# All eight heads of a chunked RWKV-7 recurrence in one sequence of chunks per pass, on one Trainium2 core

## The chip, the core and the metric

The program runs on one core of a Trainium2 chip. The core's engines work side by side, each with its own in-order queue: TensorE (PE in the profile, its weight loads PEld) multiplies matrices into PSUM; VectorE (DVE), ScalarE (ACT) and GpSimd (POOL) do the element-wise work; SP issues the DMAs between HBM and the on-chip memory (SBUF). They wait for each other through semaphores. The metric is the device time of one execution in microseconds.

## What is computed

Two layers' worth of branches share one input: an RWKV-7 recurrence (eight heads of 64) and a sliding-window attention (eight query heads, two key heads, window 128). Both are gated, merged and added to the input. The prompt has 2048 tokens; eight single-token samples go through the same weights.

```python
mod = (jax.nn.silu(c) @ w_ada + b_ada)[:, None, :]
shift, scale, gate = jnp.split(mod, 3, axis=-1)
h = rms_norm(x, norm_g) * (1.0 + scale) + shift
u = h @ w_in
...
def step(S, inp):
    r_t, w_t, k_t, v_t, kk_t, a_t = inp
    sa = jnp.einsum('bhvk,bhk->bhv', S, -kk_t)
    S = (S * w_t[:, :, None, :] + sa[..., None] * (kk_t * a_t)[:, :, None, :]
         + v_t[..., None] * k_t[:, :, None, :])
    return S, jnp.einsum('bhvk,bhk->bhv', S, r_t)
S_fin, o = lax.scan(step, s0.astype(f32), (seq(r_h), seq(w_h), seq(k_h), seq(v_h), seq(kk), seq(a_h)))
...
y_a = o_a * jax.nn.silu(z_a)
y_b = o_b * jax.nn.silu(z_b)
merged = jax.nn.sigmoid(g_a) * (y_a @ w_o_a) + jax.nn.sigmoid(g_b) * (y_b @ w_o_b)
return x + gate * (merged @ w_out), wkv_new, shift_new, k_state, v_state
```

All of it is fp32. The recurrence is computed in chunks of 64 steps: inside a chunk the steps are solved at once by the inverse of a triangular 64x64 matrix for each head and chunk, and only the state goes from chunk to chunk.

## The kernel before

**Passes.** The tokens go in four passes of 512 columns, which are eight chunks of 64. One pass (pass 1) also carries the eight sample columns, in two pieces of 260.

**Dense tiles.** `dense` makes one tile of 128 rows of `u`. Each fp32 operand is split into a high and a low part, so a tile takes three matmuls for each of eight blocks, 24 matmuls of 128x512 in all (`mm3`, issued by `mm`, L579), into one PSUM bank of the kind d. Weight pages (`w`, 128x1024) come by DMA as high and low halves; in pass 0 the vector engines also split them. An epilogue on ScalarE or VectorE takes the tile out of the bank into a page of the kind p.

**The recurrence** runs for a group of four heads (two pairs of heads, `rwkv_group`), twice a pass:

- `prep_pair` makes the decays, the keys and the matrices of each chunk.
- `inverses` inverts the 32x32 diagonal blocks. The matrices go to HBM (`d1`) and come back as one page with a matrix a partition (`NL`, one place of the kind nl). An identity page `QL` is loaded from HBM (`in_idl`). Then 31 times a product and a sum (62 VectorE instructions) build the inverses, each step from the one before. The result goes to HBM (`d2`) in two stores and comes back in eight loads as `Q`. Four VectorE transposes make `T11` from it; then come two bursts of 64 32x32 matmul records each, with a copy (`YT`) between them, which fill the off-diagonal blocks.
- The chain goes over the eight chunks: matmuls with `W` (the state into the chunk, 128x64), a copy, matmuls with `Q` (64x64) and those inside the chunk (`within`), copies, matmuls with `BK` (the new state), and sums that make the state of the next chunk. The results gather in two PSUM banks `ops` of the kind g. After the eighth chunk they are split and normed.

**The order.** The code is run once to record all operations with what they read and write (`do` L538, `mm` L579, `mms` L597, `tr` L604, `dma` L613 are the lines that the profile names). `schedule` then lists them for the engines. A key orders them: the number of the dense tile at which an operation was recorded, times six, minus a lead from the table `LEADS`; the lowest key that is ready and has its places goes first. Places are counted by `CAPS`: 75 pages of SBUF (p), 11 s, 14 t, 8 weight pages (w), one nl, three dense PSUM banks (d) and five others (g). `places` gives an operation a place only if the operations recorded ahead of it can still get theirs:

```python
if b.first > front and int(live[b.kind][front:b.first].max()) + k >= caps[b.kind]:
    return None
```

So at a point where the recorded program itself fills all pages, nothing recorded later may take one. What comes out is one fixed list for each engine, and the engines follow it in order.

**What surrounds it.** In the main loop a pass records the first group's recurrence (`rwkv(0)`), then all of the attention (`attention()`, with its dense tiles kb, vb, q and zb), then the second group's (`rwkv(1)`), then the gates, the merge and the output tiles. Ahead of pass 0, `ada` makes the modulation: a group of columns either with split operands (matmuls of 18 columns) or whole in fp32 (9 columns, `whole`), by the table `ADA`.

Of the kernel before, what the change touches and what calls it, by code (L numbers as in the profile page):

```python
# [18 lines left out]
CH = 512  # L19
# [68 lines left out]
def _constants():  # L88
# [19 lines left out]
CAPS = {"p": 75, "s": 11, "t": 14, "w": 8, "nl": 1, "d": 3, "g": 5}  # L108
LEADS = {
    "prep": (2490.0, 3436.9, 460.9, 3438.6),  # L110
    "inv": (2996.1, 5954.0, 5871.1, 5871.1),
    "chain": (3475.6, 3475.6, 3475.6, 3475.6),
    "gn": (2855.6, 4741.8, 4539.0, 2629.7),
    "wd": (2207.5, 3240.1, 1705.2, 3248.2),
    "norm": (4852.3, 820.0, 820.0, 820.0),
    "att": (4680.1, 4726.2, 4352.4, 4642.8),
    "sample": (1285.3, 1285.3, 1562.2, 1562.2),
    "bias": (2948.2, 5008.5, 5008.5, 5008.5),
    "h": (3088.9, 3088.9, 3088.9, 3109.5),
    "x": (209.4, 253.7, 253.7, 253.7),  # L120
# [388 lines left out]
def hybrid_step_kernel(ctx: ExitStack, tc: tile.TileContext, A, O):  # L509
# [152 lines left out]
    xst = K([128, 8, NB], "xst")  # L662
# [3 lines left out]
    dma(xst, A["xsT"])  # L666
# [21 lines left out]
    sct = K([128, 8, 18], "sct", F32R)  # L688
    sc32 = K([128, 8, 9], "sc32")
# [129 lines left out]
    us = K([128, len(ORDER), NB], "us")  # L819
    kprev = [K([128, 128], f"kprev{i}", F32R) for i in range(4)]  # L820
# [86 lines left out]
    def dense(key, epi):  # L907

        wt = early.pop(key, None) or weights("w_in", INDEX[key])
        for c0, n in st["segs"]:  # L910
# [194 lines left out]
    def rwkv_group(q, g, rkv, lw, lx):  # L1105
# [616 lines left out]
```

## Time and profile before

| | us |
|---|---|
| median of 2 runs | 1904.93 |
| lowest, highest | 1904.24, 1905.62 |
| the profiled execution | 1904.95 |
| its span from first to last instruction | 1903.1 |

A row of the lines names the source line, the engine, the operation, the tile written and those read, the shape of the stationary operand (for matmuls), the output's shape, the count, then busy us and mean ns of one, and last the idle time of the engine in front of them with what ended it. A row of a timeline has the start, the time to the end of the last one, and how many; in brackets the engine's idle time ahead of it. Names have lost their numbers there: `p<-p,nl` is a page written from a page and from nl. fp32 matmuls with 32x32 and 64x64 operands leave two records each.

### The profile page before, as it was taken

The page shows a single profiled execution, that of the slowest core. Times are in us where ns is not written, and L with a number is a line of the kernel's source. Part 1 is how long each engine was busy: PE and PEld are TensorE (multiplying, and loading weights), DVE is VectorE, ACT ScalarE, POOL GpSimd, SP SyncE. Part 2 cuts the span into 40 slices and gives each one's busy share as a digit, 9 for nine tenths or more (in the row PEclk, how much of TensorE's full clock was granted, in tenths as well). Part 3 has the DMA queues.
Part 4 walks back from the last instruction along what each step waited for, and adds up shares of the span by engine and source line. Part 5 has one row for each costly group of instructions (what it writes and reads, how often), then busy time and mean ns, then how long its engine had stood idle before and what let it go on. Part 6 is the DMA issues. An engine that isn't in the chain of part 4 may idle for free.

```text
span 1903.1 us, 32620 instructions
## 1 busy us (share of the span) xinstructions
PE 1807.5 (95%) x12544; PEld 1444.5 (76%) x12544; DVE 1302.0 (68%) x3138; ACT 798.5 (42%) x1605; POOL 93.9 (5%) x170
## 2 busy tenths in 40 slices
PE   6899999999999799899999999999999999999999
PEld 2667666677799778798998786677788787677787
DVE  8889979459377869792835795964563885894351
ACT  6667545353157355323504544521422562651300
POOL 0000210000000001010000100100000000100000
PEclk9999999999999899999999999999999999999999
DMA  9475537667845413453676453145467454236355
GB/s 335 175 265 213 172 110 273 222 231 283 320 158 175 145 68 102 161 189 118 211 245 201 145 183 119 67 157 186 150 228 249 158 177 141 72 125 194 113 192 187
DMA packets 162456, 343.20 MB, mean 180 GB/s; under 512 B 65485, under 2 KB 69246, under 8 KB 162300
## 3 DMA queue, kind: packets, MB, share of 16 engines
q1 hardware_dynamic: 162300, 341.11, 52.6%
q8 instruction: 99, 1.62, 0.3%
q14 instruction: 57, 0.47, 0.1%
HBM read 263.09 MB, written 77.96 MB: 179 GB/s over the span
## 4 chain that ended last, share of the span: by engine, by line
PE 48%; DVE 18%; ACT 4%; DMA 2%; issue 1%; SPq 1%; DVEq 0%; ACTq 0%
PE d L579 39%; DVE p L538 17%; PE g L597 5%; ACT p L538 3%; PE g L579 2%; PE g L604 2%; ACT L538 1%; DMA p<-in_xT 1%; DMA p<-d 1%; SPq L613 1%; DMA p<-in_swkv 0%; DVE t L538 0%; DMA w<-lo_w_in 0%; DVE s L538 0%; DMA d<-p 0%
## 5 line engine op out<-in xcount | busy, mean ns | idle before, releaser
L579 PE MATMUL d<-p,w 128*128 128x512 f32 (+1 forms) x7080 | 1457.4, 356 | 27.4 <-DVE w L538 15.8
L579 PEld LDWEIGHTS d<-p,w 128*128 128x128 f32 x7080 | 1140.5, 190 | 229.6 <-DVE w L538 26.8
L538 DVE TENSOR_TENSOR p<-p,p 128x512 fp32r<-128x512 f32 (+4 forms) x597 | 358.4, 624 | 33.8 <-ACT p L538 21.8
L597 PE MATMUL g<-p,p 128*64 128x64 f32 (+6 forms) x3952 | 229.1, 245 | 19.4 <-DVE p L538 16.6
L597 PEld LDWEIGHTS g<-p,p 128*64 128x64 f32 (+4 forms) x3952 | 174.7, 144 | 85.8 <-DVE p L538 27.0
L538 ACT COPY p<-g 64x128 f32<-64x128 f32 (+4 forms) x339 | 124.0, 377 | 138.9 <-PE g L597 89.9
L538 ACT CAST p<-p 128x512 fp32r<-128x512 f32 (+2 forms) x201 | 121.5, 621 | 135.6 <-DVE p L538 132.6
L538 ACT ACT_TABLE_LOAD x109 | 139.8, 1283 | 22.9 <-PE g L579 20.4
L538 ACT ACTIVATE p<-d 128x512 f32<-128x512 f32 (+1 forms) x120 | 61.4, 512 | 209.0 <-PE d L579 208.6
L538 DVE TENSOR_TENSOR p<-g,s 64x128 f32<-64x128 f32 (+1 forms) x124 | 40.5, 326 | 141.4 <-PE g L597 136.8
L538 DVE TENSOR_TENSOR p<-p,nl 128x2 f32<-128x2 f32 (+30 forms) x248 | 126.9, 512 | 8.9 <-DMA p<-in_idl 3.7
L538 ACT ACTIVATE p<-d,vec 128x511 f32<-128x511 f32 (+1 forms) x65 | 38.9, 603 | 214.8 <-PE d L579 178.5
L538 DVE SCALAR_TENSOR_TENSOR p<-d,modt,p 128x512 f32<-128x512 f32 (+2 forms) x40 | 25.7, 644 | 124.7 <-PE d L579 115.1
L538 ACT ACTIVATE p<-p 128x512 f32<-128x512 f32 (+2 forms) x161 | 98.1, 633 | 17.4 <-DVE p L538 9.7
L538 DVE TENSOR_TENSOR w<-w,w 128x1024 fp32r<-128x1024 f32 x58 | 70.8, 1221 | 41.2 <-PE d L579 23.5
L579 PE MATMUL g<-p,blocks 128*128 128x512 f32 x202 | 81.8, 436 | 17.5 <-ACT p L538 11.0
L538 ACT CAST w<-w 128x1024 fp32r<-128x1024 f32 x59 | 61.9, 1050 | 83.7 <-PE d L579 51.6
L538 DVE SCALAR_TENSOR_TENSOR p<-p,d 128x512 f32<-128x512 f32 (+1 forms) x120 | 69.3, 579 | 36.9 <-PE d L579 35.8
L538 DVE TENSOR_TENSOR p<-g,cst 64x256 f32<-64x256 f32 (+1 forms) x192 | 88.6, 507 | 3.9 <-PE g L597 3.1
L538 DVE TENSOR_REDUCE p<-p 128x1 f32<-128x2 f32 (+30 forms) x248 | 86.7, 349 | 5.3
L604 PE MATMUL g<-cst,p 128*128 128x128 f32 (+1 forms) x457 | 74.3, 285 | 8.3 <-DVE p L538 7.5
L604 PEld LDWEIGHTS g<-cst,p 128*128 128x128 f32 (+1 forms) x457 | 54.8, 144 | 31.2 <-DVE p L538 12.2
(159 smaller groups left out, 1060.2 us busy)
## 6 DMA issues: line engine op xcount, KB each, us to landing
w<-hi_w_in SPq DMA_DIRECT2D x129, 512.0 KB, 3.6
w<-lo_w_in SPq DMA_DIRECT2D x129, 512.0 KB, 4.5
w<-in_w_in SPq DMA_DIRECT2D x43, 512.0 KB, 4.8
hi_w_in<-w SPq DMA_DIRECT2D x43, 512.0 KB, 3.5
lo_w_in<-w SPq DMA_DIRECT2D x43, 512.0 KB, 4.2
p<-in_xT SPq DMA_DIRECT2D x64, 256.0 KB, 5.8
p<-in_w_ada SPq DMA_DIRECT2D x48, 256.0 KB, 5.5
w<-hi_w_o SPq DMA_DIRECT2D x24, 512.0 KB, 3.6
```

Of the source, the lines that this page charges most:

```text
L538: lambda e: getattr(ENG[e], engs[e])(res(out), *(res(x) for x in a), **{n_: res(v) for n_, v in k.items()}),
L579: pr.rec({"pe": mm_cost(out, lhsT, rhs)}, lambda e: nc.tensor.matmul(res(out), res(lhsT), res(rhs), **k), [out], [lhsT, rhs], table=(part( ...
L597: nc.tensor.matmul(res(out), res(lhsT), res(rhs), **k)
L604: pr.rec({"pe": 2 * _free_size(in_) / 2400.0 + 0.003}, lambda e: nc.tensor.transpose(res(out), res(in_), res(idn)), [out], [in_, idn], tab ...
L613: lambda e: nc.sync.dma_start(out=res(out), in_=res(in_)),
```

## The change

- `rwkv_group` becomes three functions. `rwkv_prepare` is the preparation and the inverses of one group. `rwkv_chain` runs one chain over both groups: each of a chunk's three groups of matmuls now holds four pairs of heads; the banks `ops` hold four chunks of two pairs each and are split after every fourth chunk. `rwkv_norm` is the norm at the end.
- A pass records both groups' preparation, then one chain. `STAGES` says for each pass whether the attention is recorded behind it (RA) or ahead of it (AR, pass 2).
- `CAPS` gives 77 pages instead of 75. Pages that were fixed (the sample's tiles, the modulation's inputs) are now taken from these. The four last key tiles kept for the next pass are made anew from one page (`klast`).
- `LEADS` has two numbers for each pass. `ADA` takes the column groups in another order, with two of them whole. In pass 0 the matmuls of a dense tile take all high weights first and all low ones last, from the seventeenth tile on (`INORDER`); output tiles keep the old order.

```diff
-CAPS = {"p": 75, "s": 11, "t": 14, "w": 8, "nl": 1, "d": 3, "g": 5}
+CAPS = {"p": 77, "s": 11, "t": 14, "w": 8, "nl": 1, "d": 3, "g": 5}
...
-    "prep": (2490.0, 3436.9, 460.9, 3438.6),
-    "inv": (2996.1, 5954.0, 5871.1, 5871.1),
-    "chain": (3475.6, 3475.6, 3475.6, 3475.6),
+    "prep": (2430.9, 2430.9, 4278.4, 1221.9, 4278.4, 4278.4, 3438.6, 4278.4),
+    "inv": (2996.1, 2996.1, 5811.5, 5811.5, 5933.5, 5890.4, 5890.4, 5890.4),
+    "chain": (3475.6, 3475.6, 3475.6, 3202.9, 7297.1, 7297.1, 3457.1, 3475.6),
...
-ADA = ((2, False), (3, False), (0, True), (1, False))
+ADA = ((0, False), (2, True), (1, False), (3, True))
 EARLY, PLACE = 1, 3
-KORDER = True
-MIDDLE = True
+INORDER = 16
+STAGES = ('RA', 'RA', 'AR', 'RA')
...
-    kprev = [K([128, 128], f"kprev{i}", F32R) for i in range(4)]
+    klast = K([128, 128], "klast")
...
-        if KORDER:
+        if st["q"] > 0 or len(st["mm"]) < INORDER or mov is st["ms"]:
...
-    def rwkv_group(q, g, rkv, lw, lx):
+    def rwkv_prepare(q, g, rkv, lw, lx):
 
         n = 2 * q + g
         gr = {"W": [], "BK": [], "bv": [], "NS": [], "NI": [], "pc": Sm([128, 2, NC_]), "d1": d1s[n % 2], "d2": d2s[n % 2]}
@@ -1112,54 +1116,72 @@
             for i in range(2):
                 prep_pair(gr, i, 2 * g + i, *rkv[2 * g + i], lw, lx)
         with at(LEAD["inv"]):
-            Q = inverses(gr)
+            gr["Q"] = inverses(gr)
+        return gr
+
+    def rwkv_chain(grs):
+
         pr.key = line[0] * 6.0 - LEAD["chain"]
-        ps_ = slice(2 * g, 2 * g + 2)
-        We = [[w[0][0], w[0][1]] for w in gr["W"]]
-        Wo = [[w[1][0], w[1][1]] for w in gr["W"]]
-        BK, NI = gr["BK"], gr["NI"]
+        pairs = range(4)
+        of = lambda name, i: grs[i // 2][name][i % 2]
+        sides = ((lo, 0, "XE"), (hi, 1, "XO"))
         with after(last()):
-            copy(XE[0][lo, :, 0, :], Sst[lo, ps_, :], "dve/pool")
-            copy(XO[0][hi, :, 0, :], Sst[hi, ps_, :], "dve/pool")
-        both = lambda h, c: gr["pc"][h, :, c].unsqueeze(2).to_broadcast([64, 2, 64])
-        ops = [G([128, 512]) for _ in range(2)]
-        sides = ((lo, We, XE), (hi, Wo, XO))
+            for g in range(2):
+                for h, e, x in sides:
+                    copy(grs[g][x][0][h, :, 0, :], Sst[h, 2 * g:2 * g + 2, :], "dve/pool")
+        X = lambda x, i, c: grs[i // 2][x][c // 4][:, i % 2, c % 4, :]
+        parts = [[P([128, CH], F32R) for _ in range(2)] for _ in pairs]
+        ops = None
 
         def within(c):
 
-            return [(ops[i][h, c * 64:c * 64 + 64], x[c // 4][h, i, c % 4, :], NI[i][h, c, :],
-                     dict(start=False, stop=(c == NC_ - 1), skip_group_check=True))
-                    for i in range(2) for h, w, x in sides if c >= 0]
+            t = c % 4 * 64
+            return [(ops[i // 2][h, i % 2, t:t + 64], X(x, i, c)[h], of("NI", i)[h, c, :],
+                     dict(start=False, stop=(c % 4 == 3), skip_group_check=True)) for i in pairs for h, e, x in sides]
 
         for c in range(NC_):
             c4, cc = divmod(c, 4)
-            ct_ = slice(c * 64, c * 64 + 64)
-            ps = G([128, 2, 64])
-            mms([(ps[h, i], w[i][c4][:, cc, 0:64], x[c4][:, i, cc, :], FULL) for i in range(2) for h, w, x in sides]
-                + [(ops[i][h, ct_], x[c4][:, i, cc, :], w[i][c4][:, cc, 64:128],
-                    dict(start=(c == 0), stop=False, skip_group_check=True)) for i in range(2) for h, w, x in sides])
-            gs = Sm([128, 2, 64])
+            t = cc * 64
+            if cc == 0:
+                ops = [G([128, 2, 256]) for _ in range(2)]
+            ps = G([128, 4, 64])
+            mms([(ps[h, i], of("W", i)[e][c4][:, cc, 0:64], X(x, i, c), FULL) for i in pairs for h, e, x in sides]
+                + [(ops[i // 2][h, i % 2, t:t + 64], X(x, i, c), of("W", i)[e][c4][:, cc, 64:128],
+                    dict(start=(cc == 0 and i % 2 == 0), stop=False, skip_group_check=True)) for i in pairs for h, e, x in sides])
+            page = P([128, 8, 64])
+            gs, sp = page[:, 0:4, :], page[:, 4:8, :]
             copy(gs, ps)
-            sp = Sm([128, 2, 64])
-            for h, w, x in sides:
-                mul(sp[h], x[c4][h, :, cc, :], both(h, c), "dve/pool")
-            ps = G([128, 2, 64])
-            mms([(ps[h, i], Q[i][h, c, :], gs[h, i], FULL) for i in range(2) for h, w, x in sides] + within(c - 1))
-            copy(XE[c4][lo, :, cc, :], ps[lo])
-            copy(XO[c4][hi, :, cc, :], ps[hi])
-            ps = G([128, 2, 64])
-            mms([(ps[h, i], BK[i][c4][:, cc, 64 * e:64 * e + 64], x[c4][:, i, cc, :], FULL)
-                 for i in range(2) for e, (h, w, x) in enumerate(sides)] + (within(c) if c == NC_ - 1 else []))
+            for g in range(2):
+                for h, e, x in sides:
+                    mul(sp[h, 2 * g:2 * g + 2, :], grs[g][x][c4][h, :, cc, :],
+                        grs[g]["pc"][h, :, c].unsqueeze(2).to_broadcast([64, 2, 64]), "dve/pool")
+            ps = G([128, 4, 64])
+            mms([(ps[h, i], of("Q", i)[h, c, :], gs[h, i], FULL) for i in pairs for h, e, x in sides]
+                + (within(c - 1) if cc > 0 else []))
+            for h, e, x in sides:
+                for g in range(2):
+                    copy(grs[g][x][c4][h, :, cc, :], ps[h, 2 * g:2 * g + 2, :])
+            ps = G([128, 4, 64])
+            mms([(ps[h, i], of("BK", i)[c4][:, cc, 64 * e:64 * e + 64], X(x, i, c), FULL) for i in pairs for h, e, x in sides]
+                + (within(c) if cc == 3 else []))
             n4, nn = divmod(c + 1, 4)
-            for h, w, x in sides:
-                add(x[n4][h, :, nn, :] if c + 1 < NC_ else Sst[h, ps_, :], ps[h], sp[h])
-
+            for h, e, x in sides:
+                for g in range(2):
+                    ps_ = slice(2 * g, 2 * g + 2)
+                    add(grs[g][x][n4][h, :, nn, :] if c + 1 < NC_ else Sst[h, ps_, :], ps[h, ps_, :], sp[h, ps_, :])
+            if cc == 3:
+                cols = slice(256 * c4, 256 * c4 + 256)
+                for i in pairs:
+                    big, small = parts[i]
+                    copy(big[:, cols], ops[i // 2][:, i % 2])
+                    sub(small[:, cols], ops[i // 2][:, i % 2], big[:, cols].f32())
         out = []
-        for i in range(2):
-            h, l = P([128, CH], F32R), P([128, CH], F32R)
-            copy(h, ops[i])
-            sub(l, ops[i], h.f32())
-            out.append((h, l))
+        for g in range(2):
+            out += rwkv_norm(g, grs[g], parts[2 * g:2 * g + 2])
+        return out
+
+    def rwkv_norm(g, gr, out):
+
         pr.key = line[0] * 6.0 - LEAD["gn"]
...
-        def rwkv(g):
-            for p in (2 * g, 2 * g + 1):
-                rkv[p] = tuple([shifted((n, p)) for n in "rkv"])
-            ots.extend(rwkv_group(q, g, rkv, lw, lx))
+        def rwkv():
+            grs = []
+            for g in range(2):
+                st["half"] = g
+                for p in (2 * g, 2 * g + 1):
+                    rkv[p] = tuple([shifted((n, p)) for n in "rkv"])
+                grs.append(rwkv_prepare(q, g, rkv, lw, lx))
+            st["half"] = 0
+            ots.extend(rwkv_chain(grs))
 
...
-        if MIDDLE:
-            rwkv(0)
-            yb = attention()
-            rwkv(1)
-        else:
-            rwkv(0)
-            rwkv(1)
-            yb = attention()
+        for stage in STAGES[min(q, 3)]:
+            if stage == "A":
+                yb = attention()
+            else:
+                rwkv()
+        st["half"] = 0
```

**TensorE, pass 0, the second group's inverse, before.** The 32x32 matmuls are the bursts; `d` are dense banks, `w` weight pages, `p` pages; `blocks` is a constant for norms. Between this and the first group's second burst (row 803) stand 529 rows of other work.

```order
L579 MATMUL d0_218<-p23_145_635,w3_722_3511 128x512
L579 MATMUL d0_218<-p24_149_653,w2_712_3428 128x512
L597 MATMUL g3_224<-p53_728_3529,p5_506_2356 32x32 x16
L597 MATMUL g3_224<-p53_728_3529,p39_566_2718 32x32 x16
L579 MATMUL d0_218<-p26_150_660,w2_712_3428 128x512
L579 MATMUL d0_218<-p24_149_653,w3_722_3511 128x512
L579 MATMUL d0_218<-p72_151_663,w2_712_3428 128x512
L579 MATMUL d0_218<-p73_155_672,w2_712_3428 128x512
L579 MATMUL d0_218<-p72_151_663,w3_722_3511 128x512
L579 MATMUL d2_220<-p56_129_589,w4_727_3521 128x512
L597 MATMUL g1_222<-p50_715_3452,p13_732_3585 32x32 x16
L597 MATMUL g1_222<-p41_716_3457,p13_732_3585 32x32 x16
```

The second burst of a group stands some dense rows behind the first.

**TensorE, pass 0, both groups' inverses, now** (rows 704 to 713).

```order
L579 MATMUL d1_210<-p22_136_609,w1_412_2012 128x512
L597 MATMUL g2_214<-p23_423_2080,p3_219_959 32x32 x16
L597 MATMUL g2_214<-p23_423_2080,p28_257_1176 32x32 x16
L597 MATMUL g3_215<-p52_416_2028,p3_425_2117 32x32 x16
L597 MATMUL g3_215<-p51_417_2034,p3_425_2117 32x32 x16
L597 MATMUL g4_216<-p23_431_2237,p69_302_1403 32x32 x16
L597 MATMUL g4_216<-p23_431_2237,p76_370_1746 32x32 x16
L597 MATMUL g0_212<-p3_429_2221,p76_435_2279 32x32 x16
L597 MATMUL g0_212<-p28_430_2225,p76_435_2279 32x32 x16
L579 MATMUL d2_211<-p12_110_521,w2_408_1973 128x512
```

The four bursts of both groups (g2 and g3 the first group's, g4 and g0 the second's) stand in one row, and the next dense row writes bank d2_211.

**VectorE, pass 0, the second loop's beginning before** (rows 578 to 586): `nl0` and the two pages beside it are the loop; the rest is other work of that time.

```order
L538 TENSOR_TENSOR p36_619_2984<-p62_614_2970,p68_618_2980 128x512
L538 TENSOR_TENSOR p19_621_2991<-p42_604_2938,nl0_592_2874 128x2
L538 TENSOR_REDUCE p42_604_2938<-p19_621_2991 128x1
L538 TENSOR_TENSOR p19_621_2991<-p42_604_2938,nl0_592_2874 128x2x3
L538 TENSOR_REDUCE p42_604_2938<-p19_621_2991 128x2
L538 TENSOR_TENSOR p19_621_2991<-p42_604_2938,nl0_592_2874 128x2x4
L538 TENSOR_REDUCE p42_604_2938<-p19_621_2991 128x2
L538 TENSOR_TENSOR w6_624_3005<-w4_512_2402,w2_569_2733 128x1024
L538 TENSOR_TENSOR p19_621_2991<-p42_604_2938,nl0_592_2874 128x3x5
```

The first loop's transposes are rows 470 to 481, about a hundred rows ahead.

**VectorE, pass 0, the first group's transposes and the second loop's beginning now** (rows 385 to 390), and **its end** (rows 450 to 456).

```order
L538 MEMSET nl0_413_2015 128x32
L538 STREAM_TRANSPOSE p23_423_2080<-p52_416_2028 32x256 x2
L538 STREAM_TRANSPOSE p23_423_2080<-p51_417_2034 32x256 x2
L538 TENSOR_TENSOR p28_428_2158<-p23_426_2119,nl0_413_2015 128x2
L538 TENSOR_REDUCE p23_426_2119<-p28_428_2158 128x1
```

The loop follows the transposes at once. Its page p23_426 lies in the place of p23_423, which the first burst reads.

```order
L538 MEMSET p3_429_2221 32x8x32
L538 MEMSET p28_430_2225 32x8x32
L538 STREAM_TRANSPOSE p23_431_2237<-p3_429_2221 32x256 x2
L538 STREAM_TRANSPOSE p23_431_2237<-p28_430_2225 32x256 x2
L538 CAST p69_434_2276<-p0_383_1827 64x512
L538 TENSOR_TENSOR p69_434_2276<-p0_383_1827,p69_434_2276 64x512
L538 SCALAR_TENSOR_TENSOR p23_433_2274<-p23_433_2274,d2_211 128x512
```

Behind its 62 instructions (rows 388 to 449) come the second group's transposes, and three rows later the instruction that reads bank d2_211.

More of the change, by code (lines that the diff above doesn't have):

```diff
@@ L687, in hybrid_step_kernel @@
     zero(eps[:, 2:3], KAPPA)
-    sct = K([128, 8, 18], "sct", F32R)
-    sc32 = K([128, 8, 9], "sc32")
+    sct = P([128, 8, 18], F32R)
+    sc32 = P([128, 8, 9])
     tht = Sm([128, 8, 9])
@@ L825, in hybrid_step_kernel @@
            for i in range(2)]
-    st = {"mm": [], "q": 0}
+    st = {"mm": [], "ms": None, "q": 0, "half": 0}
     class Lead:
         def __getitem__(self, name):
-            return LEADS[name][min(st["q"], 3)]
+            return LEADS[name][2 * min(st["q"], 3) + st["half"]]
     LEAD = Lead()
@@ L863, in make_h @@
         xs, acc = [], None
+        if sample:
+            n = len(ORDER)
+            page = P([128, n + 16, NB])
+            st.update({"us": page[:, 0:n], "xst": page[:, n:n + 8], "so": page[:, n + 8:n + 12], "sob": page[:, n + 12:n + 16]})
+            with after(*st.get("gate", ())):
+                dma(st["xst"], A["xsT"])
         for k in range(8):
@@ L916, in dense @@
                 if c0 + n > CH:
-                    copy(us[:, INDEX[key], :], ps[:, m:n])
+                    copy(st["us"][:, INDEX[key], :], ps[:, m:n])
         step_line()
@@ L1214, in queries, with keys @@
         return out
-    def keys(x):
-        out = [P([128, CH], F32R) for _ in range(4)]
+    def keys(x, out):
         for e, h in enumerate((lo, hi)):
@@ L1306, in sample_rwkv @@
     def sample_rwkv(lw):
+        us = st["us"]
         prev = Sm([128, 13, NB])
@@ L1355, in sample_rwkv @@
         mul(bv, ps, v)
-        o = K([128, 4, NB], "so")
+        o = st["so"]
         idv = Sm([128, 64])
@@ L1561, in attention @@
                     dma(O["kwp"], x[:, CH - 128:CH])
-                kk = keys(x)
+                kprev = []
+                if q > 0:
+                    before = P([128, 4, 128], F32R)
+                    kprev = keys(klast, [before[:, i, :] for i in range(4)])
+                kk = keys(x, [P([128, CH], F32R) for _ in range(4)])
+                copy(klast, x[:, CH - 128:CH], "dve/pool")
             x = plain(("vb", 0))
@@ L1571, in attention @@
                     qn.append(queries(x))
-            here = line[0] * 6.0
+            here = line[0]
             zb = [gate_z(("zb", p)) for p in range(4)]
-            pr.key = here - LEAD["att"]
+            pr.key = here * 6.0 - LEAD["att"]
             bt = [[P([128, 2, 256]) for _ in range(2)] for _ in range(2)]
@@ L1580, in attention @@
             for n in range(4):
-                attend(q, n, qn, kk, vt, bt, zb)
-            for i in range(4):
-                copy(kprev[i], kk[i][:, CH - 128:CH], "dve/pool")
+                st["half"] = n // 2
+                pr.key = here * 6.0 - LEAD["att"]
+                attend(q, n, qn, kk, kprev, vt, bt, zb)
             copy(vprev, vt[:, 3], "dve/pool")
@@ L1586, in attention @@
             return zb
-        if MIDDLE:
-            rwkv(0)
-            yb = attention()
-            rwkv(1)
-        else:
-            rwkv(0)
-            rwkv(1)
-            yb = attention()
+        for stage in STAGES[min(q, 3)]:
[3 more added lines that the diff above has]
+                rwkv()
+        st["half"] = 0
         if sample:
@@ L1627, in hybrid_step_kernel @@
                 hk = make_h(q + 1)
-        ms = [merge(j, *gates[j], ya, yb, segs) for j in range(8)]
+        ms = st["ms"] = [merge(j, *gates[j], ya, yb, segs) for j in range(8)]
         for j in range(8):
```

32 lines of the change are left out of this document (15 added, 17 removed).

## The prediction

> **What bounds the kernel now.** I read the cores' line first, then the page, then the lines by form, and then timelines of the places that the change touches.
>
> ```profile
> core 0: 1903.1 us, clock 0.984
> PE 1807.5 (95%) x12544; PEld 1444.5 (76%) x12544; DVE 1302.0 (68%) x3138; ACT 798.5 (42%) x1605; POOL 93.9 (5%) x170
> PE 48%; DVE 18%; ACT 4%; DMA 2%; issue 1%; SPq 1%; DVEq 0%; ACTq 0%
> L579 PE MATMUL d<-p,w 128*128 128x512 f32 x4248 | 1082.3, 402 | 26.3 <-DVE w L538 15.8 <-DVE p L538 4.4 <-ACT w L538 3.2
> L597 PE MATMUL g<-p,p 32*32 32x32 f32 x1024 | 25.4, 209 | 12.8 <-DVE p L538 12.7
> L538 DVE TENSOR_TENSOR p<-p,nl 128x2 f32<-128x2 f32 (+30 forms) x248 | 126.9, 512 | 8.9 <-DMA p<-in_idl 3.7
> L538 DVE TENSOR_REDUCE p<-p 128x1 f32<-128x2 f32 (+30 forms) x248 | 86.7, 349 | 5.3
> ```
>
> TensorE is the bound: 95% busy, all other engines far below. The time is what it has to do plus what it waits, so a stretch in which it gets nothing is added whole. The one long serial piece beside it is the inverse: one per group of four heads, eight in all, 62 VectorE instructions that each need the one before. (126.9 + 86.7) / 8 = 26.7 us of VectorE apiece. Today TensorE waits only 12.8 us in all for its 32x32 matmuls, which need these inverses, since dense matmuls stand between them.
>
> **The inverse and its trip through memory.** Three views of before: the windows (PE, PEld, DVE, ACT, POOL busy, clock, DMA share, GB/s), then the timeline of pass 2, then VectorE's and TensorE's of pass 1, where TensorE did run dry, the slowest trip, and the load of the identity page.
>
> ```profile
> 1272.20:1301.10 28.90, 28.90 (x126) 23.46 (x125) 26.79 (x62) 3.60 (x6) 0.00 (x0) 1.00 0.53 184
> 658.50:669.00 10.50, 9.43 (x150) 8.67 (x151) 6.54 (x25) 4.46 (x12) 0.00 (x0) 0.51 0.10 16
> 1156.89 0.75 PE L579 MATMUL d<-p,w 128*128 128x512 f32 x1 [1.82 <-DVE p L538]
> 1157.57 1.92 PE L597 MATMUL g<-p,p 32*32 32x32 f32 x64
> ...
> 1272.20 0.16 DVE L538 TENSOR_TENSOR p<-p,nl 128x2 f32<-128x2 f32 x1 [3.67 <-DMA p<-in_idl]
> 1300.39 0.69 DVE L538 TENSOR_REDUCE p<-p 128x16 f32<-128x512 f32 x1
> 1300.67 12.66 PE L579 MATMUL d<-p,w 128*128 128x512 f32 x54
> 1301.11 1.26 SPq L613 DMA_DIRECT2D d<-p  x2
> 1306.62 3.94 SPq L613 DMA_DIRECT2D p<-d  x8
> 1310.73 1.90 DVE L538 STREAM_TRANSPOSE p<-p 32x256 f32<-32x256 f32 x4 [8.99 <-DMA p<-d]
> ...
> 651.74 0.69 DVE L538 TENSOR_REDUCE p<-p 128x16 f32<-128x512 f32 x1
> 660.76 0.44 DVE L538 STREAM_TRANSPOSE p<-p 32x256 f32<-32x256 f32 x1 [0.22 <-DMA p<-d]
> ...
> 644.78 4.22 PE L579 MATMUL d<-p,w 128*128 128x260 f32 x34
> 658.50 0.31 PE L597 MATMUL g<-p,p 32*32 32x32 f32 x2 [9.50 <-DVE p L538]
> ...
> 1732.98 0.69 DVE L538 TENSOR_REDUCE p<-p 128x16 f32<-128x512 f32 x1
> 1749.91 1.83 DVE L538 STREAM_TRANSPOSE p<-p 32x256 f32<-32x256 f32 x4 [15.59 <-DMA p<-d]
> ...
> p<-in_idl SPq DMA_DIRECT2D x8, 256.0 KB, 4.9
> ```
>
> To be seen: a loop that VectorE does alone takes 28.9 us (1272.20 to 1301.08). TensorE was busy through all of it with dense work. From its end to the end of the four transposes, without which no 32x32 matmul starts, go 11.5 us in pass 2 (1301.08 to 1312.63: store, loads, transposes), 8.8 us in pass 1 (652.43 to 661.20) and 18.1 us at worst (1733.67 to 1751.74). Where no dense row stood ready (pass 1), TensorE waited 9.50 us. Dense matmuls go at 12.66 / 54 = 0.234 us each (512 columns) or 4.22 / 34 = 0.124 us (260).
>
> **The change part by part.**
>
> *The second inverse of each pass loses its cover: about +172 us.* Both groups are now prepared one behind the other, then one chain takes both. By the order, TensorE has in passes 0, 1 and 2 not one dense matmul between the first group's first 32x32 burst and the second group's, and 17 in pass 3; VectorE does the whole second loop in this stretch. Before, 529 TensorE rows of dense and attention stood there in pass 0. The scheduler has no choice in it: 77 places is exactly the peak of live pages at this point, the three dense banks are full, and a dense tile's epilogue gets no page until the recurrence is past its peak. In the order of pass 0, TensorE's first dense row behind the bursts writes bank d2_211, which VectorE reads for the tile before in row 456, behind the second group's transposes (452 and 453).
>
> What stands in series, counted from the end of the first group's loop:
> - its trip, 8.8 to 11.5 us; I take 10.0, between the quiet and the busy one;
> - half of its burst, and then the load of the identity page (4.9 us to landing), which goes into a place that this burst reads: about 6 (bounds 1.5, if that load finds another place early, and 7);
> - the second loop, 28.9 (26.7, if nothing of VectorE's comes between, is the lower bound);
> - its trip, again 10.0.
>
> That is 54.9 us, four times 219.6. TensorE has work in it: the bursts, 3.8 us a pass (two of 64 records at 1.92), 15.2 in all, and what dense work is left when the first loop ends. From banks and weight pages, the order allows at most 32 matmuls in pass 0, 25 of 260 columns in pass 1, 26 in pass 2 and 69 in pass 3: 32 x 0.234 + 25 x 0.124 + 95 x 0.234 = 32.8. So 219.6 - 15.2 - 32.8 = 171.6 us of new idle time.
>
> *Fewer turns between array shapes: -22 us.* Both chains' matmuls now go in one group, so 96 groups stand where 192 stood; over the whole program the order has 542 changes of shape before and 320 now, 111 pairs fewer. What a pair costs shows in the chain of pass 2:
>
> ```profile
> 1159.42 4.21 PE L579 MATMUL d<-p,w 128*128 128x512 f32 x9
> ...
> 1166.58 1.20 PE L579 MATMUL d<-p,w 128*128 128x512 f32 x4
> 1167.71 0.69 PE L597 MATMUL g<-p,p 128*64 128x64 f32 x16
> 1168.32 0.73 PE L579 MATMUL d<-p,w 128*128 128x512 f32 x2
> 1168.98 0.45 PE L597 MATMUL g<-s,p 64*64 64x64 f32 x8
> ```
>
> From start to start, four dense matmuls take 1.13 us and two take 0.66: 0.20 us over 0.234 apiece each time. A pair is 0.20, and 111 of them 22 us. They lie on TensorE's own path, so the gain is whole (bounds 0, should the longer steps give it back, and 24).
>
> *The chain's steps: 0.* Behind a step's last two groups of matmuls stand four copies or sums of 64x128 where two stood, but between its groups are three, four and five dense matmuls where two, three and four were.
>
> ```profile
> L538 DVE TENSOR_TENSOR p<-g,s 64x128 f32<-64x128 f32 (+1 forms) x124 | 40.5, 326 | 141.4 <-PE g L597 136.8
> ```
>
> VectorE waits for TensorE there, 136.8 us in all, so the dense matmuls cover the step today. Two sums more are 0.65 us, one dense matmul more 0.23: without slack a step costs 0.42 us, 32 steps 13 us (bounds 0 and 13).
>
> *Modulation columns: +2.* The order has 16 matmuls of 18 columns fewer and 8 whole fp32 ones of 9 more, of two records each:
>
> ```profile
> L579 PE MATMUL d<-p,sct 128*18 128x512 f32 x80 | 24.7, 431 | 15.5 <-ACT p L538 14.0 <-DVE p L538 1.4
> L579 PE MATMUL d<-p,sc 128*9 128x512 f32 x16 | 7.4, 593 | 0.1
> ```
>
> At 0.43 us a record, 8 x 2 x 0.43 = 6.9 against 16 x 0.234 = 3.7 is +3. Part of it lies in the 15.5 us that TensorE waits there anyhow: 0 to 3.
>
> *What goes.* The 12.8 us before the old bursts are inside the new waits: -13. With the low halves last in pass 0 from the seventeenth tile on, part of the 15.8 us behind split weights goes: 0 to -15.8, I take half, -8. Sample pages, the key page and their copies move among vector engines with slack: 0 (bounds -3 and +3).
>
> *The clock behind a wait: +2.* After the 9.50 us wait the granted clock was 0.51 for the next 10.5 us (the window above), and behind a 1.82 us wait nine dense matmuls took 4.21 us, where 2.1 is usual. Four such restarts cost 2 us each, but most of the new waits end in bursts, which are short, and before's own restarts there are gone: 0 to 8, taken as 2. The Trainium skill (TensorE: Matmul & The Clock Gate, section "Why this matters for your kernels") says that one gap of over some 3 us puts TensorE back to half rate. The row agrees, but shows a longer half-rate stretch than the window of some 3.4 us that the page gives; by the page, an estimate of 4 x 1.7 = 7 us would stand where I have 2.
>
> Sum against the profiled execution, 1904.95 us (0.02 over the median of the runs): 1904.95 + 172 - 22 + 0 + 2 - 13 - 8 + 2 = **2038 us**.
>
> The Trainium skill (DMA: Bandwidth & Descriptors, section "Anatomy of one DMA — SWDGE (gpsimd) path") gives a fixed cost of about 2.0 us a transfer on that path: two in a row, with transposes, would be an estimate of some 6.5 us where I took 10.0, and the sum would be some 28 us lower. The trips above are all longer, so they decide.
>
> **The rivals.**
>
> *Hidden after all (not slower).* If TensorE were some 40 us behind VectorE whenever the first group's transposes are done, it would eat that backlog during the second loop. Then only turns and small terms count: 1904.95 - 22 + 2 - 13 - 8 = 1864 us; with some 10 us a pass left uncovered, 1904. It decides at (22 + 13 + 8 - 2) / 4 = 10 us of idle time per pass. For it: the window at 1272.20 shows just such cover today. Against it: what comes before the first burst in TensorE's queue must have been run, since in pass 0 the load that waits for its last dense row (704) stands ahead of the inverse's loads on SP; and behind the burst nothing dense is queued.
>
> *Shorter waits.* Quiet trips (8.8), the identity page early (1.5), and some 30 dense matmuls more left per pass: 4 x 48.0 - 15 - 33 - 28 = 116 instead of 172, and with all weight waits gone 1904.95 + 116 - 22 - 13 - 8 = 1978 us. For it: TensorE's dense rows are slowed behind each earlier wait, so more is left.
>
> *Longer waits.* The trip took 18.1 us where other loads were queued. One such trip a pass: 4 x 8.1 = 32, and restarts at half clock with 8 instead of 2, and turns as before by the longer steps: 2038 + 32 + 6 + 19 = 2095 us.
>
> *Chain steps that show.* The waits as forecast and the 13 us of the steps: 2051 us. For it: VectorE's sums go behind other work in its queue; against it: five dense matmuls, 1.2 us, stand there, and two pairs of sums are 1.3.
>
> **How the numbers follow.** Forecast 0.52 (1995 to 2075 for itself), shorter waits 0.20, longer 0.10, chain steps 0.10, hidden 0.08. The first four are all slower by over 2%, which is about what a measurement of this kernel can tell from no change (38 us). Of the last, 0.03 is faster by more than that, 0.04 within it, and 0.01 slower. The range of 1975 to 2095 leaves out the hidden case and the outer parts of the shorter and the longer waits, 2 in 10 together.
>
> **What would show it.** In the profile after: four gaps on TensorE, each split into a piece of some 10 us and one of some 40, ended by VectorE's transposes, and the idle time before 32x32 matmuls up from 12.8 to over 150 us; VectorE busy with the loop alone inside each; TensorE's busy share near 88%. The turns are right if four dense matmuls between groups still take about 1.13 us and the shape changes are 222 fewer. It is wrong if TensorE's row shows dense work inside the second loop, if the loops overlap the first group's trip, or if a gap is under 25 us.

## The result and the profile after

| | before | changed |
|---|---|---|
| median of 2 runs, us | 1904.93 | 2004.25 |
| lowest, highest, us | 1904.24, 1905.62 | 2003.91, 2004.59 |
| the profiled execution, us | 1904.95 | 2003.91 |

The changed kernel takes 1.0522 times as long (95% interval 1.0496 to 1.0547), 99 us more. The forecast was 2038 us, with a range of 1975 to 2095.

The cores' line of the changed kernel, its page's row of busy times, and two rows of its lines by form:

```profile
core 0: 2002.1 us, clock 0.947
```

```profile
PE 1776.3 (89%) x12544; PEld 1447.0 (72%) x12544; DVE 1290.0 (64%) x3152; ACT 785.4 (39%) x1607; POOL 97.5 (5%) x146
```

```profile
L579 PE MATMUL d<-p,w 128*128 128x512 f32 x4248 | 1053.3, 400 | 10.1 <-DVE w L538 6.3 <-POOL w L538 2.0 <-ACT p L538 0.7
L597 PE MATMUL g<-p,p 32*32 32x32 f32 x1024 | 34.5, 229 | 163.6 <-DVE p L538 158.7 <-ACT p L538 4.7
```

The books close on TensorE (by the spans of the two profiled executions). Its idle time (span less busy) went from 1903.1 - 1807.5 = 95.6 us to 2002.1 - 1776.3 = 225.8, which is 130.2 more. In front of the 32x32 matmuls alone it grew from 12.8 to 163.6, by 150.8; all other waits together shrank by 20.6. And TensorE was busy 31.2 us less, though its 32x32 matmuls took 9.1 more (34.5 after 25.4). So 150.8 - 20.6 - 31.2 = 99.0, the difference of the spans.

One of the four waits, in pass 2, in the timeline of the changed kernel: the rows of VectorE and SP on which the reading rests, and then those of TensorE. Rows between them are left out.

```profile
1285.79 0.69 DVE L538 TENSOR_REDUCE p<-p 128x16 f32<-128x512 f32 x1
1286.96 1.26 SPq L613 DMA_DIRECT2D d<-p  x2
1293.12 3.77 SPq L613 DMA_DIRECT2D p<-d  x8
1297.76 0.43 DVE L538 STREAM_TRANSPOSE p<-p 32x256 f32<-32x256 f32 x1 [0.52 <-DMA p<-d]
1297.96 0.38 SPq L613 DMA_DIRECT2D p<-in_idl  x1
1302.49 0.16 DVE L538 TENSOR_TENSOR p<-p,nl 128x2 f32<-128x2 f32 x1 [4.30 <-PE g L597]
1329.69 0.69 DVE L538 TENSOR_REDUCE p<-p 128x16 f32<-128x512 f32 x1
1330.40 1.23 SPq L613 DMA_DIRECT2D d<-p  x2
1334.03 3.93 SPq L613 DMA_DIRECT2D p<-d  x8
1339.00 0.43 DVE L538 STREAM_TRANSPOSE p<-p 32x256 f32<-32x256 f32 x1 [0.85 <-DMA p<-d]
...
1296.14 0.24 PE L597 MATMUL g<-p,p 32*32 32x32 f32 x2 [1.66 <-DVE p L538]
1300.57 1.91 PE L597 MATMUL g<-p,p 32*32 32x32 f32 x62 [0.29 <-ACT p L538]
1336.37 0.31 PE L597 MATMUL g<-p,p 32*32 32x32 f32 x2 [33.89 <-DVE p L538]
```

This is the sequence that was forecast: the first loop's trip, the bursts, the second loop, its trip. One step differs in this pass: the identity page is loaded beside the burst (issued at 1297.96), and what the second loop waits for last is the end of the first group's second burst at 1302.48. In the other three passes it waits for the identity page, 3.84, 2.30 and 7.10 us. TensorE has nothing from 1302.48 to 1336.37. The windows of the second loop in the passes 0 to 3 (PE, PEld, DVE, ACT, POOL busy, clock, DMA share, GB/s) show VectorE at it nearly alone; TensorE's 1.91 us in pass 1 are the rest of the first group's second burst:

```profile
231.12:258.90 27.78, 0.46 (x16) 0.32 (x12) 25.68 (x62) 1.25 (x4) 0.30 (x1) 0.50 0.00 1
717.93:745.70 27.77, 1.91 (x62) 1.78 (x62) 25.67 (x62) 1.28 (x5) 0.30 (x1) 0.50 0.00 1
1302.49:1330.30 27.81, 0.00 (x0) 0.00 (x0) 25.71 (x62) 1.26 (x4) 0.30 (x1) 0.50 0.00 1
1693.17:1721.00 27.83, 0.44 (x2) 0.01 (x1) 25.73 (x62) 0.00 (x0) 0.00 (x0) 0.56 0.11 38
```

Before, the one such window quoted had TensorE busy for all of its 28.90 us.

### The profile page after: what moved, and what is told of

Same layout as the page of the kernel before. It is cut to its first block, busy times and chain, and to the rows that moved or that the text cites. A ratio compares the mean times of both kernels' runs of the same rounds, so it can differ in the third digit from the quotient of the medians.

```text
span 2002.1 us, 32602 instructions
## 1 busy us (share of the span) xinstructions
PE 1776.3 (89%) x12544; PEld 1447.0 (72%) x12544; DVE 1290.0 (64%) x3152; ACT 785.4 (39%) x1607; POOL 97.5 (5%) x146
## 3 DMA queue, kind: packets, MB, share of 16 engines
q1 hardware_dynamic: 162300, 341.11, 49.5%
## 4 chain that ended last, share of the span: by engine, by line
PE 63%; DVE 24%; ACT 5%; DMA 4%; issue 3%; SPq 1%; POOL 0%; DVEq 0%; ACTq 0%; POOLq 0%
PE d L579 51%; DVE p L538 23%; PE g L597 8%; ACT p L538 3%; PE g L579 3%; PE g L604 2%; ACT L538 1%; SPq L613 1%; DMA d<-p 1%; DMA p<-in_xT 1%; DMA p<-d 1%; DVE w L538 1%; DMA p<-in_idl 0%; DMA nl<-d 0%; POOL w L538 0%
## 5 line engine op out<-in xcount | busy, mean ns | idle before, releaser
L579 PE MATMUL d<-p,w 128*128 128x512 f32 (+1 forms) x7080 | 1421.2, 354 | 12.5 <-DVE w L538 6.3
L538 DVE TENSOR_TENSOR p<-p,p 128x512 fp32r<-128x512 f32 (+6 forms) x587 | 346.7, 617 | 81.3 <-ACT p L538 74.7
L597 PE MATMUL g<-p,p 64*64 64x64 f32 (+5 forms) x4512 | 238.5, 245 | 169.2 <-DVE p L538 163.2
L597 PEld LDWEIGHTS g<-p,p 128*64 128x64 f32 (+4 forms) x4512 | 191.8, 147 | 228.5 <-DVE p L538 180.4
L538 ACT COPY p<-g 64x128 f32<-64x128 f32 (+6 forms) x383 | 128.5, 358 | 232.8 <-PE g L597 175.3
L538 ACT CAST p<-p 128x512 fp32r<-128x512 f32 (+2 forms) x191 | 114.2, 612 | 134.1 <-DVE p L538 129.0
L538 DVE TENSOR_TENSOR p<-p,nl 128x2 f32<-128x2 f32 (+30 forms) x248 | 125.3, 505 | 23.0 <-DMA p<-in_idl 13.2
L538 DVE TENSOR_TENSOR p<-g,p 64x128 f32<-64x128 f32 (+3 forms) x224 | 64.8, 330 | 107.8 <-PE g L597 83.7
L538 ACT ACTIVATE p<-p 128x512 f32<-128x512 f32 (+2 forms) x161 | 97.9, 633 | 27.9 <-DVE p L538 18.5
L538 DVE TENSOR_REDUCE p<-p 128x1 f32<-128x2 f32 (+31 forms) x252 | 88.7, 352 | 5.4
```

The costliest lines, as they stand in the source:

```text
L538: lambda e: getattr(ENG[e], engs[e])(res(out), *(res(x) for x in a), **{n_: res(v) for n_, v in k.items()}),
L579: pr.rec({"pe": mm_cost(out, lhsT, rhs)}, lambda e: nc.tensor.matmul(res(out), res(lhsT), res(rhs), **k), [out], [lhsT, rhs], table=(part( ...
L597: nc.tensor.matmul(res(out), res(lhsT), res(rhs), **k)
```

## The experiments

The question was no longer whether the waits are there, but what makes them: the loop itself, the two preparations standing back to back, the one chain that needs both inverses, or the pages.

### 1. Leaving out the second loop, in the changed kernel and in the one before

```diff
-        gr = {"W": [], ...
+        gr = {"g": g, "W": [], ...
...
-        for t in range(1, 32):
+        for t in range(1, 32 if gr["g"] == 0 else 2):
```

> The changed kernel without 60 of the 62 instructions of the second group's inverse in each pass (only the first step is left, so the second group's result is not the reference's); everything else stands in the same order. Theory A (the second loop lost its cover): each of the four waits of 32 to 34 us loses the loop's 27.7 us, 4 x 27.7 = 111, so about 1893 us, and the idle time before 32x32 matmuls falls from 163.6 to about 53 us. Theory B (the loop is not what TensorE waits for; the wait is set by pages, banks or other VectorE work and only ends with the loop): the waits shrink by less than half, 1950 us or more.

Measured: 1901.26 us, 0.9988 of the kernel before (0.9979 to 0.9997), so 103 us less than with the loop, where A said 111. The idle time before 32x32 matmuls, in the lines of this run, is down to 56:

```profile
L597 PE MATMUL g<-p,p 32*32 32x32 f32 x1024 | 34.6, 231 | 56.0 <-DVE p L538 51.2 <-ACT p L538 4.7
```

> The same left out of the kernel before. Theory A: the second loops lie beside dense work there, so next to nothing is gained: 1890 to 1905 us (only part of the 12.8 us before the 32x32 matmuls can go). Theory B' (the loops were always on the path in part, through VectorE's other work): 30 us or more are gained, under 1875 us.

Measured: 1904.19 us, 1.0004 of the kernel before (0.9993 to 1.0016): no gain. The same 60 instructions a pass cost 103 us in one kernel and nothing in the other. So the loop holds TensorE up in the changed kernel only. Theory A holds that far (its 1893 us were 8 too low), B and B' fall.

### 2. Two chains behind both preparations

```diff
-            ots.extend(rwkv_chain(grs))
+            for g in range(2):
+                ots.extend(rwkv_chain(grs, g, g + 1))
```

`rwkv_chain` then takes the groups from g to g + 1 only.

> The changed kernel with two chains of four heads, one behind the other, after both preparations; all else as changed. Theory A (the cover is lost because the two preparations are recorded back to back): the four waits of some 33 us stay, and the turns come back: 2004 + 22 to 31, 2026 to 2035 us. Theory C (the one chain over eight heads makes the wait, since its first step needs both inverses): the first chain runs during the second loop, the waits shrink by 10 us or more each, and the time is under 1985 us.

Measured: 2050.28 us, 1.0774 (1.0756 to 1.0792). The idle time before 32x32 matmuls is 160.0 us, close to the changed kernel's 163.6.

```profile
L597 PE MATMUL g<-p,p 32*32 32x32 f32 x1024 | 32.8, 223 | 160.0 <-DVE p L538 155.0 <-ACT p L538 4.8
```

So it isn't the merging of the chains as such (theory C) that makes TensorE wait: with two chains it waits as long. But the merging is worth more than A had it (22 to 31), namely 46 us. The two timelines of pass 2 show why, first of the two chains, then of the one:

```profile
1379.73 0.69 PE L597 MATMUL g<-p,p 128*64 128x64 f32 x16
1380.34 0.97 PE L579 MATMUL d<-p,w 128*128 128x512 f32 x3
1381.24 0.45 PE L597 MATMUL g<-p,p 64*64 64x64 f32 x8
1381.62 0.96 PE L579 MATMUL d<-p,w 128*128 128x512 f32 x3
```

```profile
1349.03 1.15 PE L597 MATMUL g<-p,p 128*64 128x64 f32 x32
1350.12 0.97 PE L579 MATMUL d<-p,w 128*128 128x512 f32 x3
1351.02 0.68 PE L597 MATMUL g<-p,p 64*64 64x64 f32 x16
1351.63 1.20 PE L579 MATMUL d<-p,w 128*128 128x512 f32 x4
```

From start to start, 16 small matmuls take 0.61 us and 32 take 1.09: two groups of 16 cost 0.13 more than one of 32. 8 take 0.38 and 16 take 0.61: 0.15 more. The dense rows behind a group keep their 0.20 over 0.234 apiece (three take 0.90). So a pair of turns costs about 0.35 us, 0.20 in the dense rows and 0.13 to 0.15 in the small ones. TensorE is busy 1811.3 us here and 1776.3 in the changed kernel; the trace has 198 changes of shape more, or 99 pairs: 35.0 / 99 = 0.35 a pair. The other 11 us are waits: one of 12.09 is new, behind pass 1's chain, and the rest is a little shorter together.

The Trainium skill (TensorEngine Tiling (Array Packing), section "Key Properties") says that a change of tiling mode drains TensorE; it gives no price. The 0.35 us are this kernel's price for a change and back. They would fit a drain; that they are one, no row shows.

### 3. The attention between the two preparations, one chain behind them

```diff
-        for stage in STAGES[min(q, 3)]:
...
+        for g in range(2):
...
+            grs.append(rwkv_prepare(q, g, rkv, lw, lx))
+            if g == 0:
+                yb = attention()
+        ots.extend(rwkv_chain(grs))
```

> The changed kernel with the attention recorded between the two preparations, and the one chain over eight heads behind them. In the order dense matmuls stand between the first group's bursts and the second's again in every pass. Theory A: the waits before 32x32 matmuls fall from 163.6 us to about what they were (13 to 40), while the fewer turns stay: 2004 - 125 to 150, 1855 to 1880 us, faster than before. Theory D (the one chain costs as much as it saves, by longer steps or by pages that are held longer): 1900 us or more, with the idle time elsewhere.

Measured: 1990.07 us, 1.0456 (1.0440 to 1.0471). A miss: dense rows stand between the bursts again, and still TensorE waits 125.3 us for its 32x32 matmuls. (D's time fits, but the idle time isn't elsewhere.) In pass 0 it had worked off these rows long before the second inverse came:

```profile
L597 PE MATMUL g<-p,p 32*32 32x32 f32 x1024 | 31.2, 223 | 125.3 <-DVE p L538 124.2 <-ACT p L538 1.0
269.70 14.80 PE L579 MATMUL d<-p,w 128*128 128x512 f32 x63
314.71 0.31 PE L597 MATMUL g<-p,p 32*32 32x32 f32 x2 [30.22 <-DVE p L538]
```

63 dense matmuls are under three tiles; then nothing for 30 us. So theory A, as "the preparations stand back to back", is not the cause, only one way to get it. What the programs that wait have in common may be few spare pages. Counted over the recorded operations of each program, the kernel before has at most 52 of its 75 pages alive at once. The changed one has 68 of 77, mainly since the matrices of both groups live until the one chain has read them, and a_rar 73. Spare are 23, 9 and 4. Dense work recorded later may run ahead only as far as spare pages take its results (the rule in `places`). That is theory P.

### 4. Pages

```diff
-CAPS = {"p": 75, "s": 11, "t": 14, "w": 8, "nl": 1, "d": 3, "g": 5}
+CAPS = {"p": 61, "s": 11, "t": 14, "w": 8, "nl": 1, "d": 3, "g": 5}
```

> The kernel before with 61 SBUF pages instead of 75. Its recorded program has at most 52 pages alive at once, the changed kernel's 68: so 23 of 75 are spare before, 9 of 77 with the change, and 9 here. Theory P (the spare pages are the cover: dense work recorded later can only run ahead as far as they reach, and the one chain takes 16 of them because both groups' matrices live at once): waits like those of the changed kernel appear in a program that has two chains and the attention between them, 1990 to 2060 us, 80 us or more of it idle before 32x32 matmuls. Theory A (the cover is lost only because the two preparations stand back to back): the attention still stands between the bursts, at most 1930 us.

Measured: 2046.80 us, 1.0756 (1.0740 to 1.0772). Nothing of the change is in this kernel, only its shortage of pages, and its TensorE waits 142.9 us before 32x32 matmuls, where it waited 12.8 with 75 pages. From its lines by form and its timeline of pass 0, second group:

```profile
L597 PE MATMUL g<-p,p 32*32 32x32 f32 x1024 | 32.3, 226 | 142.9 <-DVE p L538 142.9
```

```profile
339.28 4.20 PE L579 MATMUL d<-p,w 128*128 128x512 f32 x17
385.68 0.31 PE L597 MATMUL g<-p,p 32*32 32x32 f32 x2 [42.20 <-DVE p L538]
...
351.78 0.16 DVE L538 TENSOR_TENSOR p<-p,nl 128x2 f32<-128x2 f32 x1 [1.63 <-DMA p<-in_idl]
377.92 1.02 DVE L538 TENSOR_TENSOR p<-p,nl 128x512 f32<-128x512 f32 x1
```

TensorE runs dry at 343.5, and the whole second loop (351.8 to 379.7) lies in its wait. That is the changed kernel's wait, in a kernel with the order of before. In the passes 1 to 3 it is not: there 69.5 of the 79.7 us stand in front of the first group's first burst. Theory P holds that far; theory A gave at most 1930.

The other way round, the changed kernel with five pages fewer and five more:

```diff
-CAPS = {"p": 77, "s": 11, "t": 14, "w": 8, "nl": 1, "d": 3, "g": 5}
+CAPS = {"p": 82, "s": 7, "t": 13, "w": 6, "nl": 1, "d": 3, "g": 5}
```

(a_p72 has only p changed, to 72. a_p82 takes the room from weight pages and small tiles, and what these do alone was not run.)

> The changed kernel with 82 pages instead of 77; the room comes from two weight pages (6 instead of 8), four s and one t tiles that are spare. Theory P: each page more lets about one dense tile of 24 x 0.234 = 5.6 us run in each wait, so up to 4 x 5 x 5.6 = 112 us less, and at least a third of that: 1890 to 1965 us. Theory A: the order of the groups is as before, 1990 to 2010 us.

> The changed kernel with 72 pages, five fewer. Theory P: 40 to 112 us more, 2045 to 2115 us, in longer waits before 32x32 matmuls and before the loops. Theory A: 2000 to 2015 us.

| pages | spare | us | ratio to before (95%) | idle before 32x32 | of it in passes 0, 1, 2, 3 |
|---|---|---|---|---|---|
| 72 | 4 | 2063.94 | 1.0842 (1.0824 to 1.0860) | 198.0 | 48.6, 44.4, 67.2, 37.8 |
| 77 | 9 | 2004.25 | 1.0522 (1.0496 to 1.0547) | 163.6 | 49.5, 39.5, 38.9, 35.8 |
| 82 | 14 | 1965.82 | 1.0334 (1.0319 to 1.0350) | 123.2 | 47.3, 28.9, 9.9, 37.1 |

```profile
L597 PE MATMUL g<-p,p 32*32 32x32 f32 x1024 | 36.5, 236 | 198.0 <-DVE p L538 194.2 <-ACT p L538 3.6
```

```profile
L597 PE MATMUL g<-p,p 32*32 32x32 f32 x1024 | 31.0, 221 | 123.2 <-DVE p L538 121.8 <-ACT p L538 1.3
```

(The rows are those of 72 and of 82 pages.) Five pages fewer cost 60 us and five more save 38; the waits before 32x32 matmuls moved by 34.4 and 40.4 of them. P's sign and rough size hold in the sum, though 1965.82 lies just outside its 1890 to 1965, and A's "no change" falls. But the gain is not even. It lies in the passes 1 and 2, while the waits of the passes 0 and 3 hardly move. With 82 pages, between the two groups' bursts of pass 2 and before the second group's first burst of pass 0:

```profile
1292.01 20.21 PE L579 MATMUL d<-p,w 128*128 128x512 f32 x86
1320.79 0.31 PE L597 MATMUL g<-p,p 32*32 32x32 f32 x2 [8.57 <-DVE p L538]
...
268.26 0.31 PE L597 MATMUL g<-p,p 32*32 32x32 f32 x2 [33.46 <-DVE p L538]
```

In pass 2, 86 dense matmuls run where none stood with 77 pages. In pass 0 the wait is 33.5 us where it was 33.3. Counted in the programs' fixed lists, 74 to 77 of the 77 pages (79 to 82 of the 82) are in use during the long wait of every pass, so pages are short in the passes 0 and 3 too; but why five more bought nothing there no run shows. The Trainium skill (Perfetto Trace Analysis, section "Optimization Strategy") says that one gap that repeats on the engine that should be saturated can mean that SBUF or PSUM has no room for the next tile. The runs agree for the passes 1 and 2 (67.2, 38.9 and 9.9 us in pass 2 with 72, 77 and 82 pages).

### 5. The attention between the preparations, with more pages

> The attention between the two preparations, the one chain behind them (as in a_rar, which has 73 pages alive and 4 spare), with the 82 pages of a_p82: 9 spare. Theory P: of a_rar's 1990 us, 40 to 110 go: 1880 to 1950 us. If it is under 1900 us it beats both kernels, since the chain over eight heads keeps its gain of some 36 us on TensorE. Theory A, which a_rar left unexplained, gives no change: 1980 us or more.

Measured: 1896.17 us, 0.9963 (0.9952 to 0.9973). It is 94 us less than a_rar, which has four spare pages where nine are here (and, as in a_p82, fewer weight pages and small tiles). Of the waits before 32x32 matmuls 55 us are gone; 70.2 are left, in two stops of 33 us in passes 0 and 1:

```profile
L597 PE MATMUL g<-p,p 32*32 32x32 f32 x1024 | 23.7, 202 | 70.2 <-DVE p L538 69.4 <-ACT p L538 0.8
```

So the attention between the preparations does help, once there are pages for it: with the same 82, the changed kernel's order takes 1965.82.

To spare more, the bonus goes through HBM (into four new tiles `bvds`):

```diff
-        gr["bv"].append(r)
+        dma(bvds[p], r)
+        gr["bv"].append(bvds[p])
...
-            add(ot, ot, gr["bv"][i], "dve/pool")
+            bv = P([128, CH])
+            with after(last()):
+                dma(bv, gr["bv"][i])
+            add(ot, ot, bv, "dve/pool")
```

> As r_p82, and the bonus pages (r_k, k, r and v summed, four pages that wait for the norm through the whole chain) go to HBM and come back at the norm: in the passes 1 to 3 four pages more, in pass 0 two, are spare at the chain. Theory P: of the two waits of 33 us that r_p82 still has in passes 0 and 1, 10 to 30 us go in all: 1866 to 1888 us, faster than before by 1 to 2%. Without it, or if the extra DMAs stand in the way on SP: 1895 us or more.

Measured: 1884.98 us, 0.9899 (0.9883 to 0.9916). That is 1.0% less than before. The interval does not reach 1, but the gain is under the 2% that the prediction took as about what can be told from no change. It is the lower end of the gain over r_p82 that was named. TensorE is busy 1760.8 us, 46.7 less than before, and waits 52.2 for 32x32 matmuls. The long stop of pass 1 went from 33.0 to 11.8 us; that of pass 0 didn't shrink (33.4, now 36.3). The page's row, and that of the waits (total, times, longest; for all matmuls of line 597):

```profile
PE 1760.8 (94%) x12544; PEld 1433.5 (76%) x12544; DVE 1282.8 (68%) x3167; ACT 794.9 (42%) x1623; POOL 70.0 (4%) x115
```

```profile
PE g L597 <- DVE p L538: 54.7, 18, 36.3
```

So the one chain can be a gain for TensorE where its pages are found in another way.

### 6. The side edits alone

```diff
-ADA = ((2, False), (3, False), (0, True), (1, False))
+ADA = ((0, False), (2, True), (1, False), (3, True))
+INORDER = 16
...
-        if KORDER:
+        if st["q"] > 0 or len(st["mm"]) < INORDER or mov is st["ms"]:
```

> The kernel before with only two side edits of the change: the new order of the modulation's column groups (two of them whole) and the low weights last in pass 0 from the seventeenth tile on. By the prediction's terms +2 - 8 = -6 us, 1897 us. If they are larger than I took them (the changed kernel's idle time outside the 32x32 matmuls is 20 us less than before): 1880 to 1890 us. If they do nothing: 1901 to 1905 us.

Measured: 1909.57 us, 1.0031 (1.0019 to 1.0044): 6 us more, not less. A miss for all three. In its lines (which stand one further down in this kernel) the dense matmuls' waits did fall by about what was taken, 26.3 to 17.0, but the norms' matmuls (`blocks`) wait 32.1 where they waited 17.5. The first row is of before:

```profile
L579 PE MATMUL g<-p,blocks 128*128 128x512 f32 x200 | 81.8, 439 | 17.5 <-ACT p L538 11.0 <-DVE p L538 6.1
L580 PE MATMUL d<-p,w 128*128 128x512 f32 x4248 | 1078.1, 402 | 17.0 <-DVE w L539 7.1 <-DVE p L539 4.8 <-ACT p L539 2.8
L580 PE MATMUL g<-p,blocks 128*128 128x512 f32 x200 | 83.5, 444 | 32.1 <-DVE p L539 24.1 <-ACT p L539 7.3
```

Whether the columns' order or the low halves brought that wasn't tried apart.

## Why the prediction was right, and where it was off

**The second inverse loses its cover (+172 us): right in its mechanism, with stages that were off and cancelled.** Read as in pass 2 above, in all four passes:

| us | first trip | to the second loop | second loop | second trip | sum |
|---|---|---|---|---|---|
| pass 0 | 18.6 | 3.8 | 27.8 | 9.1 | 59.3 |
| pass 1 | 11.5 | 2.3 | 27.8 | 8.8 | 50.4 |
| pass 2 | 11.7 | 4.3 | 27.9 | 9.0 | 53.0 |
| pass 3 | 12.5 | 7.1 | 27.9 | 8.7 | 56.2 |
| predicted | 10.0 | 6 | 28.9 | 10.0 | 54.9 |

The sum over the passes is 218.8, where 219.6 stood. That it came so near is luck: the first trips took 14 us more than forecast over the four passes, and the other three stages 15 less together. TensorE waited 163.6 us, 151 more than before, where 172 - 13 = 159 was forecast; so it had some 55 us to do in these stretches, and 48 had been taken. The split of the gaps was off too: 10 and 40 us were named, and the long stops are 12.0, 4.8, 1.7 and 0 us before the first group's first bursts and 32 to 34 before the second group's. In the passes 1 to 3 dense work covered much of the first trip.

**Its reason was half right.** The step said that the preparations stand back to back and that 77 pages are exactly the peak of live pages. The program by itself has 68 alive; the other nine are given to work recorded later before the wait comes. That pages are refused bears on the waits, as the runs of section 4 show, but it doesn't need the two preparations to be neighbours: a_rar has them apart and waits 125 us, b_p61 has the order and the two chains of before and waits 143. With the one chain (and in e_two just as well) up to 16 more pages are alive than before, mainly because both groups' matrices are held at once. In the passes 0 and 3 of the changed kernel the loop makes the wait (a_noloop2), but that pages alone keep other work from filling it is argued: five more didn't shorten it.

**Fewer turns (-22 us): right in kind, too small by some 17.** The count was right: the traces have 542 changes of shape before and 320 now. But the step priced a pair at 0.20 us, from the dense rows alone. The small rows lose 0.13 to 0.15 more each time a group is split in two. At 0.35 a pair, 111 pairs are 39 us. Of the sum's terms it has the largest error.

**The chain's steps (0): right.** TensorE waits 4.4 us in front of 128x64 matmuls in the changed kernel, 3.3 before, and nothing in front of 64x64:

```profile
L597 PE MATMUL g<-p,p 128*64 128x64 f32 x1536 | 60.8, 226 | 4.4 <-DVE p L538 4.0 <-ACT p L538 0.2
L597 PE MATMUL g<-p,p 64*64 64x64 f32 x1024 | 38.5, 222 | 0.0
```

**The side edits (-8 and +2): wrong in sign when alone.** b_small has +6. In the changed kernel the waits outside the 32x32 matmuls are 20.6 us shorter all the same. One might think that the long stops let VectorE and ScalarE catch up. The runs speak against it: these other waits are 62.2 us in the changed kernel and 61.6 in a_noloop2, where the long stops are gone, but 81.8 in b_p61, which has long stops and the order of before (82.8 before). So they go with the changed program; which part of it does that stays open.

**The clock (+2): too small.** Granted was 0.50 in three of the four loops' windows, and the bursts behind a stop ran at this clock: the 32x32 matmuls are 9.1 us longer. All other matmuls together lost no more than before: TensorE was busy with them at half the clock for 28.5 us, where it had been 36.3.

Together: -8 for the waits, -17 for turns, -12 for the other waits, and +3 for the clock and the rest give the 34 us between 2038 and 2004. The +3 are what remains, and were not taken apart.

**The rivals.** "Hidden after all" fell in every window above. "Longer waits" named a trip of 18 us in each pass; it came once, 18.6 in pass 0. (Its 19 us for the turns that come back follow from no row; the whole 22 would make 2098.) "Shorter waits" (1978 us) took 48.0 us a pass in series, where 54.7 was measured; that the time lies between it and the forecast comes from the turns and the other waits more than from these. "Chain steps" didn't show.

## What to carry to other kernels

When work is merged so that two producers must both be done before one consumer starts, count what stays alive meanwhile. In a program whose list is laid down ahead, as here, the spare buffers limit how far the bound engine can run ahead, and that work hides the latency of everything else. Look for the place where the bound engine's rows end while its queue still has work that may not have a buffer. Then change one number, the count of buffers, up and down, and read the waits stage by stage: here it moved the passes 1 and 2 and left 0 and 3 as they were, which the total alone would have hidden. And a gain from fewer switches can be real and still be lost: here it was some 39 us against 151. It was had, with 1.0% below the old time, once room was found elsewhere.

## What the runs showed of the hardware

A change of TensorE between the 128x128 array and smaller operands and back costs 0.35 us in this kernel, of which the rows of the dense matmuls show only 0.20. A burst of 64 matmul records of 32x32 took 1.20 us in pass 3 of the changed kernel, where TensorE came from dense work and the granted clock was 1.00. In pass 2, behind short waits and with 0.50 granted, 62 of them took 1.91 us. And a trip of 256 KB through HBM and back, with four transposes, took from 8.7 to 18.6 us in one execution. In the long one SP issued other transfers between the stores and the loads (from 211.0 to 218.4), and the eight loads took it 7.06 us to issue, where they took 3.77 in pass 2:

```profile
218.47 7.06 SPq L613 DMA_DIRECT2D p<-d  x8
1689.67 1.20 PE L597 MATMUL g<-p,p 32*32 32x32 f32 x64
```
